# Stick-breaking heads: the keys' low parts queued behind a softplus' low part, and one multiplication moved to the end of a head's output

## The chip, the cores and the metric

The kernel runs on one core of a Trainium2 chip. The metric is the device time of one execution in microseconds (us). Every time below is from a run on the chip or from a hardware profile of one execution. The engines are named as in the profile: PE multiplies matrices (PEld is its weight load), DVE and ACT do elementwise work, POOL does elementwise work and masks, SP starts transfers.

## What is computed

The reference is one block of a hybrid encoder for 512 tokens and 16 learned meta tokens, 528 in all, of width 1024, in float32. A normalised input is projected once into all the parts; stick-breaking attention (8 heads of width 64) and gated linear attention (4 heads) run side by side, are merged by sigmoid gates, and a gated MLP follows. The change lies in the stick-breaking attention:

```python
z = jnp.einsum('bhqd,bhkd->bhqk', qi, k) * scale
u = jnp.where(strict, jax.nn.log_sigmoid(-z), 0.0)
tail = lax.cumsum(u, axis=3, reverse=True) - u
w = jnp.where(strict, jnp.exp(jax.nn.log_sigmoid(z) + tail), 0.0)
return jnp.einsum('bhqk,bhkd->bhqd', w, v)
```

So a head needs logits, a softplus of them, a running sum of that softplus over the keys, an exponential, and a product with the values.

## The kernel before

**Two-part numbers.** PE multiplies in a rounded format. To stay near float32, the kernel splits each operand into a high part (`h` at the end of the tile's name, a rounding copy) and a low part (`l`, the operand minus the high part), and adds up the products high by high, high by low and low by high. A high part in these heads is a CAST on DVE at L144, its low part a TENSOR_TENSOR at L145 (`split_v`). A product `z<-v0h,tri` is thus followed by its twin `z<-v0l,tri`.

**Stages.** The input is normalised; then come the four gated-linear heads, then the stick-breaking heads in four pairs (`for j in range(4)`), then the output projections and the MLP. For each pair the weights of three projections (`sk`, `sq`, `sv`: keys, queries and values, made by `sb_proj`, one pair ahead) and of four gate projections (`mg`, `go`, `mg`, `go`) arrive by transfer. ACT rounds each block of weights (L88, tile `wh_...`, 128x1024), and POOL makes its low part (L89, tile `wl_...`, 128x1024). The projections (`proj`, L113) are by far the most work on PE in this stage; the attention's own products lie between them.

**One pair.** `sb_parts` makes the operands of a pair's two heads: ACT rounds the keys and the scaled queries (`ks` L601, `qh` L603 and L605), DVE makes the low parts (`ks` L602, `ql` L604 and L606, 64x528, two of each a pair). `sb` then runs the keys in blocks of 128. First come the last 16 tokens and the first 16 for both heads together (tiles `zs`, `vs`, `ws`; `vs` is also the name of the split values), then block 3 for both heads (`z` of 288 columns), then for each head blocks 2, 1 and 0 (272, 400 and 512 columns). For a block PE makes the logits (`z`, L619), ACT takes three functions of them (`e`, L624 to L626), DVE makes the softplus (`v`, L628), POOL masks the diagonal (L632), DVE splits it (`v0h`, `v0l` for block 0), PE adds its running sum to `z` (L642) and sums it for the earlier blocks (`s`, L656), ACT takes the exponential (`w`, L646), POOL masks it, DVE multiplies in what the later blocks left over (L649) and splits the weights (`w0h`, `w0l`), and PE multiplies all weights with the values into the head's output `po` (L736 to L741). Before, that output begins with block 0, high and then low, and goes on with blocks 1, 2, 3 and the last tokens.

**What sets the order.** The program is written in the order of the text, and a list scheduler with a cost model of its own lays the instructions of all engines out in time; what it lays out is the order in which each engine then runs them, one after another. `tc.issue_after(x)` around an instruction tells it not to place that instruction ahead of x. On the chip each engine runs its list in order and waits by semaphores for operands and free buffers. So `sk`, `sq`, `sv` of the next pair and the operands of the next pair are laid out beside the second head of the pair before.

## Time and profile before

| | |
|---|---|
| median of 3 runs | 947.62 us (947.43 to 950.25) |
| the profiled execution's own time | 947.23 us |
| its span, first to last instruction | 945.5 us |
| PE busy | 920.3 us, 97% |
| DVE busy | 631.7 us, 67% |
| ACT busy | 492.3 us, 52% |
| POOL busy | 351.0 us, 37% |
| mean granted PE clock | 0.995 |

PE is busy nearly everywhere, so the time is PE's work and the moments at which PE stands still. A row of the profile's timeline has a start in us from the span's beginning, a duration in us, the engine, the line, the operation, `output<-inputs` by tile names, and shapes; `x2` says that a row stands for two instructions. A bracket at its end gives the idle time of the engine ahead of it and the instruction that ended that. The stick-breaking heads lie between about 250 and 474 us.

### The profile page before, as it was taken

How to read it: one execution, taken by the hardware profiler on the slowest of the kernel's cores; microseconds unless marked ns; L12 is line 12 of the kernel's file. 1: busy time of each engine (PE TensorE's matmuls, PEld its weight loads, DVE VectorE, ACT ScalarE, POOL GpSimd, SP SyncE). 2: the span in 40 equal slices, each digit the busy share in tenths (PEclk: the TensorE clock that was granted, in tenths of full speed). 3: DMA queues.
4: the chain of work that ended last, by engine and by line, in shares of the span. 5: the costliest groups of instructions: out<-in, count | busy, mean ns of one | idle time of the engine just before them, and what ended most of it. 6: DMA issues, size and time to landing. Idle time of an engine off the chain costs nothing.

```text
span 945.5 us, 17900 instructions
## 1 busy us (share of the span) xinstructions
PE 920.3 (97%) x7229; PEld 842.8 (89%) x7229; DVE 631.7 (67%) x1080; ACT 492.3 (52%) x934; POOL 351.0 (37%) x259
## 2 busy tenths in 40 slices
PE   7999999999999998999999998999999999999996
PEld 7999999999999997999998777999999999988785
DVE  6576858677558785887848438455544445488988
ACT  6674656556567674676663245533333333355654
POOL 5433232333355443554445331544444444101100
PEclk9999999999999999999999999999999999999998
DMA  7122222212223212221214642333333333274923
GB/s 221 46 69 68 69 68 68 68 47 72 64 73 85 62 52 68 67 82 54 73 53 122 232 141 96 101 101 90 89 90 98 102 90 90 90 267 154 266 81 123
DMA packets 129876, 93.39 MB, mean 99 GB/s; under 512 B 4080, under 2 KB 114930, under 8 KB 129794
## 3 DMA queue, kind: packets, MB, share of 16 engines
q1 hardware_dynamic: 126178, 82.55, 29.4%
q10 hardware_dynamic: 2112, 6.82, 2.0%
q0 software_dynamic: 1504, 2.88, 1.8%
q8 instruction: 57, 0.93, 0.4%
q14 instruction: 25, 0.20, 0.1%
HBM read 88.05 MB, written 4.19 MB: 98 GB/s over the span
## 4 chain that ended last, share of the span: by engine, by line
PE 86%; DVE 7%; issue 2%; ACT 2%; POOL 1%; DMA 0%; DVEq 0%; POOLq 0%; ACTq 0%
PE pt_up L113 13%; PE ga L915 12%; PE pt_gv L113 5%; PE pt_gr L113 5%; PE pt_mg L113 4%; PE pt_ms L113 4%; PE pt_go L113 4%; PE dA L1087 3%; PE dD L1087 3%; PE pt_gk L113 3%; PE wob L930 3%; PE pt_so L113 2%; PE pt_gq L113 2%; PE dB L1087 2%; PE wo L951 2%
## 5 line engine op out<-in xcount | busy, mean ns | idle before, releaser
L89 POOL TENSOR_TENSOR wl_ga<-raw_ga,wh_ga 128x1024 fp32r<-128x1024 f32 x22 | 55.3, 2518 | 74.3 <-ACT wh_ga L88 57.1
L89 POOL TENSOR_TENSOR wl_up<-raw_up,wh_up 128x1024 fp32r<-128x1024 f32 x22 | 52.9, 2407 | 79.4 <-ACT wh_up L88 79.4
L113 PE MATMUL pt_up<-h2h,wh_up 128*128 128x256 f32 (+1 forms) x352 | 73.1, 283 | 1.3 <-ACT h2h L140 1.3
L113 PE MATMUL pt_up<-h2l,wh_up 128*128 128x256 f32 (+1 forms) x352 | 73.3, 283 | 0.0
L113 PE MATMUL pt_up<-h2h,wl_up 128*128 128x256 f32 (+1 forms) x352 | 73.2, 282 | 0.0
L915 PE MATMUL ga<-h2h,wh_ga 128*128 128x512 f32 (+1 forms) x192 | 72.0, 376 | 0.7 <-ACT h2h L140 0.7
L915 PE MATMUL ga<-h2l,wh_ga 128*128 128x512 f32 (+1 forms) x192 | 72.1, 376 | 0.0
L915 PE MATMUL ga<-h2h,wl_ga 128*128 128x512 f32 (+1 forms) x192 | 72.1, 376 | 0.0
L88 ACT CAST wh_up<-raw_up 128x1024 fp32r<-128x1024 f32 x22 | 23.1, 1049 | 78.8 <-PE pt_up L113 75.0
L113 PEld LDWEIGHTS pt_up<-h2h,wh_up 128*128 128x128 f32 x352 | 56.8, 189 | 3.3 <-ACT h2h L140 1.6
L113 PEld LDWEIGHTS pt_up<-h2l,wh_up 128*128 128x128 f32 x352 | 55.5, 189 | 0.0
L113 PEld LDWEIGHTS pt_up<-h2h,wl_up 128*128 128x128 f32 x352 | 55.4, 189 | 0.0
L915 PEld LDWEIGHTS ga<-h2h,wl_ga 128*128 128x128 f32 x192 | 36.2, 188 | 7.0
L915 PEld LDWEIGHTS ga<-h2h,wh_ga 128*128 128x128 f32 x192 | 36.1, 188 | 7.0 <-ACT h2h L140 0.9
L915 PEld LDWEIGHTS ga<-h2l,wh_ga 128*128 128x128 f32 x192 | 36.1, 188 | 6.2
L1018 DVE SCALAR_TENSOR_TENSOR cy<-pt_up,cw,cy 128x511 f32<-128x511 f32 (+1 forms) x22 | 16.4, 745 | 36.5 <-ACT cy L1015 36.5
L88 ACT CAST wh_ga<-raw_ga 128x1024 fp32r<-128x1024 f32 x22 | 23.1, 1048 | 26.4 <-PE ga L915 25.2
L1018 DVE SCALAR_TENSOR_TENSOR yp<-pt_up,cw,yp 128x511 f32<-128x511 f32 (+1 forms) x22 | 16.4, 746 | 29.6 <-ACT yp L1015 29.6
L140 ACT CAST sh_p<-As 128x512 fp32r<-128x512 f32 (+1 forms) x30 | 17.4, 584 | 29.4 <-PE dB L1087 12.6
L89 POOL TENSOR_TENSOR wl_gr<-raw_gr,wh_gr 128x1024 fp32r<-128x1024 f32 x8 | 19.1, 2386 | 36.1 <-ACT wh_gr L88 27.2
L1115 POOL DMA_DIRECT2D tv<-in_w_ffn_down_dram x6 | 7.1, 1177 | 68.0 <-DVE wl_p L141 68.0
L113 PE MATMUL pt_gr<-hnh,wh_gr 128*128 128x258 f32 (+1 forms) x128 | 28.2, 294 | 0.0
(558 smaller groups left out, 3170.1 us busy)
## 6 DMA issues: line engine op xcount, KB each, us to landing
raw_up<-in_w_ffn_up_dram SPq DMA_DIRECT2D x22, 512.0 KB, 3.9
raw_ga<-in_w_ffn_gate_dram SPq DMA_DIRECT2D x22, 512.0 KB, 3.8
raw_t<-in_w_ffn_down_dram SPq DMA_DIRECT2D x10, 512.0 KB, 7.4
raw_gv<-in_w_in_dram SPq DMA_DIRECT2D x8, 512.0 KB, 3.9
raw_gr<-in_w_in_dram SPq DMA_DIRECT2D x8, 512.0 KB, 3.8
raw_mg<-in_w_in_dram SPq DMA_DIRECT2D x8, 512.0 KB, 3.8
raw_go<-in_w_gla_out_dram SPq DMA_DIRECT2D x8, 512.0 KB, 4.3
raw_ms<-in_w_in_dram SPq DMA_DIRECT2D x8, 512.0 KB, 4.0
```

What stands on the lines that cost most here:

```text
L88: act.copy(hi_out, raw)
L89: lo_eng.tensor_tensor(out=lo_out, in0=raw, in1=f32(hi_out), op=ALU.subtract)
L113: last_pr[0] = pe.matmul(dst, a[:, k, :], b[:, k, lo:hi], start=n == 0, stop=n == len(steps) - 1)
L140: act.copy(hi, src)
L915: last_mm[0] = pe.matmul(pt[:, lo:hi], a[:, k, :], b[:, k, lo:hi], start=lo == 0 and k == 0 and q == 0, stop=k == KT - 1 and q == 2, skip_ ...
L930: last_mm[0] = pe.matmul(pt, a, b, start=q == 0, stop=q == len(ops) - 1)
L951: last_mm[0] = pe.matmul(pos[i // 2][:, (i % 2) * 512 : (i % 2) * 512 + 512], m[k][:, t], w, start=k == 0 and q == 0, stop=k == 7 and q == 2)
L1018: dve.scalar_tensor_tensor(out=y[:, d:], in0=pt[:, : SEQ - d], scalar=c, in1=y[:, d:], op0=ALU.mult, op1=ALU.add)
L1087: mm[i] = pe.matmul(dsts[i], a, b, start=first and k == 0 and j == 0, stop=last and k == NP - 1 and j == 2, skip_group_check=True)
L1115: return lambda n, q, nk: pool.dma_start(out=t[:, q : q + nk, :], in_=block(s, c, q, nk), accum_op=ALU.add)
```

## The change

Two things are changed in the order of the work; no computation is added or taken out.

First, `parts` keeps the low part that it made last, and `sb` leaves behind the low part of the softplus of block 0 of its second head (`v0l`). When `sb_parts` makes the operands of the next pair, the two low parts of the keys (L602, now L606) may not be placed ahead of that `v0l`. For the first pair there is no such instruction, and nothing holds.

Second, in a head's output the second product, that with the low weights of block 0 (`w0l`), is moved to the end: `w0h`, blocks 1, 2 and 3, the last tokens, `w0l`.

```diff
@@ split_v
         dve.tensor_copy(hi, src)
-        dve.tensor_tensor(out=lo, in0=src, in1=f32(hi), op=ALU.subtract)
+        return dve.tensor_tensor(out=lo, in0=src, in1=f32(hi), op=ALU.subtract)
@@ sb_parts
                 act.copy(ks[o, hd, :], k[o])
-                dve.tensor_tensor(out=ks[n, hd, :], in0=k[o], in1=f32(ks[o, hd, :]), op=ALU.subtract)
+
+                with tc.issue_after(last_v[0].ins) if last_v[0] else ExitStack():
+                    dve.tensor_tensor(out=ks[n, hd, :], in0=k[o], in1=f32(ks[o, hd, :]), op=ALU.subtract)
@@ parts
-            split_v(hi[:rows, :n], lo[:rows, :n], src)
+            last_v[0] = split_v(hi[:rows, :n], lo[:rows, :n], src)
@@ sb
                     vp = parts(vi[:, :n], f"v{i}", nm, P, n, [P, n])
+                    low = last_v[0]
...
-                first = True
-                for i, t, wt in reversed(wts):
-                    for b in wt:
-                        pe.matmul(po[:, t - NM :], vs[:, i, hd, :], b, start=first, stop=False, skip_group_check=True)
-                        first = False
-                for b in w3:
-                    pe.matmul(po[:, 384 - NM :], vs[:, 3, hd, :], b[:, 144 * hd : 144 * hd + 144], start=False, stop=False, skip_group_check=True)
-                for b in ws:
-                    pe.matmul(po[:, 512 - NM :], vs[:16, 4, hd, :], b[:16, 32 * hd + 16 : 32 * hd + 32], start=False, stop=True, skip_group_check=True)
+                ops = [(t - NM, vs[:, i, hd, :], b) for i, t, wt in reversed(wts) for b in wt]
+                ops += [(384 - NM, vs[:, 3, hd, :], b[:, 144 * hd : 144 * hd + 144]) for b in w3]
+                ops += [(512 - NM, vs[:16, 4, hd, :], b[:16, 32 * hd + 16 : 32 * hd + 32]) for b in ws]
+                ops.append(ops.pop(1))
+                for q, (c, a, b) in enumerate(ops):
+                    pe.matmul(po[:, c:], a, b, start=q == 0, stop=q == len(ops) - 1, skip_group_check=True)
                 add_halves(hd, po, NM, 512)
             split_v(sbh[:, j, :], sbl[:, j, :], o32)
+            last_v[0] = low
```

No instruction is added or taken out on any engine. Since the scheduler lays everything out anew, the order moves on PE, DVE, ACT and POOL from the first pair's first output to the end of the stage; SP's order stays. Three places matter below. In the names `_1_` stands for the pair's second head.

The first is DVE at the end of the second pair, where the operands of the third pair (`ql`, `ks`) are made beside the second head's blocks 1 and 0. Before:

```order
L144 CAST v1h_1_4534<-v_1_4531 128x400
L707 TENSOR_TENSOR o_1_4318<-po_0_4480,lo_0_16_4491 64x512
L606 CAST ql_5003<-ql_5003 64x528 x2
L145 TENSOR_TENSOR v1l_1_4535<-v_1_4531,v1h_1_4534 128x400
L749 TENSOR_TENSOR tg<-pt_go_4951,lseg_4938 128x514
L602 TENSOR_TENSOR ks_5001<-raw_k_4594,ks_5001 64x528 x2
L628 SCALAR_TENSOR_TENSOR v_1_4561<-z_1_4554,e_1_4557 128x512
L649 TENSOR_TENSOR w_1_4540<-w_1_4540,E_1_4521 128x272
L144 CAST v0h_1_4564<-v_1_4561 128x512
L144 CAST w1h_1_4544<-w_1_4540 128x400
L145 TENSOR_TENSOR v0l_1_4565<-v_1_4561,v0h_1_4564 128x512
L145 TENSOR_TENSOR w1l_1_4545<-w_1_4540,w1h_1_4544 128x400
```

And now:

```order
L753 TENSOR_TENSOR tg<-pt_go_4951,lseg_4938 128x514
L610 CAST ql_5003<-ql_5003 64x528
L632 SCALAR_TENSOR_TENSOR v_1_4561<-z_1_4554,e_1_4557 128x512
L653 TENSOR_TENSOR w_1_4540<-w_1_4540,E_1_4521 128x272
L144 CAST w1h_1_4544<-w_1_4540 128x400
L144 CAST v0h_1_4564<-v_1_4561 128x512
L145 TENSOR_TENSOR w1l_1_4545<-w_1_4540,w1h_1_4544 128x400
L145 TENSOR_TENSOR v0l_1_4565<-v_1_4561,v0h_1_4564 128x512
L606 TENSOR_TENSOR ks_5001<-raw_k_4594,ks_5001 64x528 x2
```

The two `ks` went from ahead of the softplus `v` of block 0 to behind its low part `v0l`, and `w1h` and `w1l` came ahead of `v0l`. On ACT, at the same place, the rounding `wh_sq` (L88) went from ahead of the second function (L625) of that block's logits to behind it.

On PE, where that `v0h` and `v0l` are multiplied, the order before was this (`zs` are the third pair's first logits, which need `ks`; `pt_sq` is the query projection):

```order
L619 MATMUL zs_5029<-ql_5003,ks_5001 16x16
L113 MATMUL pt_sq_5368<-hnl,wh_sq_5364 128x272
L642 MATMUL z_1_4554<-v0h_1_4564,tri 128x512
L113 MATMUL pt_sq_5368<-hnl,wh_sq_5364 128x256
L113 MATMUL pt_sq_5368<-hnh,wl_sq_5365 128x272
L113 MATMUL pt_sq_5368<-hnh,wl_sq_5365 128x256
L113 MATMUL pt_sq_5368<-hnh,wh_sq_5364 128x272
L113 MATMUL pt_sq_5368<-hnh,wh_sq_5364 128x256
L113 MATMUL pt_sq_5368<-hnl,wh_sq_5364 128x272
L113 MATMUL pt_sq_5368<-hnl,wh_sq_5364 128x256
L642 MATMUL z_1_4554<-v0l_1_4565,tri 128x512
```

And now:

```order
L646 MATMUL z_1_4554<-v0h_1_4564,tri 128x512
L113 MATMUL pt_sq_5368<-hnh,wh_sq_5364 128x272
L113 MATMUL pt_sq_5368<-hnh,wh_sq_5364 128x256
L113 MATMUL pt_sq_5368<-hnl,wh_sq_5364 128x272
L113 MATMUL pt_sq_5368<-hnl,wh_sq_5364 128x256
L113 MATMUL pt_sq_5368<-hnh,wl_sq_5365 128x272
L113 MATMUL pt_sq_5368<-hnh,wl_sq_5365 128x256
L113 MATMUL pt_sq_5368<-hnh,wh_sq_5364 128x272
L113 MATMUL pt_sq_5368<-hnh,wh_sq_5364 128x256
L113 MATMUL pt_sq_5368<-hnl,wh_sq_5364 128x272
L646 MATMUL z_1_4554<-v0l_1_4565,tri 128x512
```

Ahead of `z<-v0h`, where the eight `zs` and one `pt_sq` stood since row 2476 of PE's list, there are now sixteen `pt_sq`; between the two `z` there are nine instead of seven; and the eight `zs` come four products behind `z<-v0l`.

The second place is DVE at the end of the third pair, where the fourth pair begins (`vs`, `ws` are its first softplus and weights). Before:

```order
L649 TENSOR_TENSOR w_1_5280<-w_1_5280,E_1_5261 128x400
L144 CAST wshs_5764<-ws_5761 16x64
L144 CAST w0h_1_5284<-w_1_5280 128x512
L145 TENSOR_TENSOR wsls_5765<-ws_5761,wshs_5764 16x64
L145 TENSOR_TENSOR w0l_1_5285<-w_1_5280,w0h_1_5284 128x512
L749 TENSOR_TENSOR tg<-pt_go_6082,lseg_6069 128x514
```

And now:

```order
L144 CAST v0h_1_5274<-v_1_5271 128x512
L145 TENSOR_TENSOR w1l_1_5255<-w_1_5250,w1h_1_5254 128x400
L145 TENSOR_TENSOR v0l_1_5275<-v_1_5271,v0h_1_5274 128x512
L606 TENSOR_TENSOR ks_5711<-raw_k_5304,ks_5711 64x528 x2
L157 TENSOR_SCALAR tg<-pt_mg_6020 128x514
L161 TENSOR_TENSOR lseg_6069<-tg,lseg_6069 128x514
L653 TENSOR_TENSOR w_1_5280<-w_1_5280,E_1_5261 128x400
L144 CAST w0h_1_5284<-w_1_5280 128x512
L145 TENSOR_TENSOR w0l_1_5285<-w_1_5280,w0h_1_5284 128x512
L632 SCALAR_TENSOR_TENSOR vs_5752<-zs_5739,es_5748 16x64
L753 TENSOR_TENSOR tg<-pt_go_6082,lseg_6069 128x514
L144 CAST vsh_5755<-vs_5752 16x64
```

`ks` moved behind `v0l` here too, and `w1l` ahead of it; the split of `ws` is no longer between `w0h` and `w0l`; the softplus `vs` and its split, which stood ahead of this stretch, now follow `w0l`. On PE the fourth pair's `zs` moved 58 rows later.

The third place is PE at the last output, that of the fourth pair's second head. Before, six products of the gate projection `pt_ms` lie between `w0h` and `w0l`, the last two of them shown:

```order
L113 MATMUL pt_ms_6519<-hnh,wh_ms_6515 128x258
L113 MATMUL pt_ms_6519<-hnh,wh_ms_6515 128x256
L736 MATMUL po_1_5998<-w0l_1_5995,vs_5726 128x512
L736 MATMUL po_1_5998<-w1h_1_5964,vs_5726 128x400
L736 MATMUL po_1_5998<-w1l_1_5965,vs_5726 128x400
L736 MATMUL po_1_5998<-w2h_1_5934,vs_5726 128x272
```

And now:

```order
L744 MATMUL po_1_5998<-w0h_1_5994,vs_5726 128x512
L744 MATMUL po_1_5998<-w1h_1_5964,vs_5726 128x400
L744 MATMUL po_1_5998<-w1l_1_5965,vs_5726 128x400
L744 MATMUL po_1_5998<-w2h_1_5934,vs_5726 128x272
L744 MATMUL po_1_5998<-w2l_1_5935,vs_5726 128x272
L744 MATMUL po_1_5998<-w3h_5795,vs_5726 128x144
L744 MATMUL po_1_5998<-w3l_5796,vs_5726 128x144
L744 MATMUL po_1_5998<-wshs_5764,vs_5726 128x16
L744 MATMUL po_1_5998<-wsls_5765,vs_5726 128x16
L744 MATMUL po_1_5998<-w0l_1_5995,vs_5726 128x512
```

The output's ten products now stand together, six rows later than before with `w0h` and eight rows later with `w0l`.

## The prediction

> **What bounds the kernel now.** I read the page's first lines, then the windows of the stick-breaking stage, then PE's waits in it, and last the timelines of the places where PE waits.

> ```profile
> span 945.5 us, 17900 instructions
> PE 920.3 (97%) x7229; PEld 842.8 (89%) x7229; DVE 631.7 (67%) x1080; ACT 492.3 (52%) x934; POOL 351.0 (37%) x259
> ...
> 250.00:474.00 224.00, 217.80 (x1683) 209.89 (x1682) 169.45 (x274) 145.59 (x285) 107.16 (x113) 0.99 0.25 68
> 360.00:362.00 2.00, 2.00 (x9) 1.91 (x10) 0.98 (x4) 0.60 (x1) 0.53 (x2) 0.50 0.77 212
> 362.00:363.00 1.00, 1.00 (x6) 1.00 (x6) 1.00 (x5) 0.00 (x0) 0.00 (x0) 0.50 0.34 100
> 363.00:364.00 1.00, 1.00 (x9) 1.00 (x8) 0.30 (x1) 0.00 (x0) 0.00 (x0) 0.86 0.00 0
> ...
> PE z L642 <- DVE v0l L145: 2.3, 1, 2.3
> PE po L736 <- DVE w0l L145: 1.4, 2, 0.9
> PE z L642 <- DVE v0h L144: 1.0, 1, 1.0
> PE zs L619 <- ACT qh L605: 0.9, 1, 0.9
> PE po L736 <- DVE w0h L144: 0.4, 1, 0.4
> ```

> The stage that the change lays out anew, 250 to 474 us, is PE's: busy 217.80 of 224.00 us, so it stands still for 6.2 us, and the five waits (total, times, longest) name 6.0 of them. The number behind POOL's in a window is the granted clock: for some 3.3 us behind 360 it was half, then 0.86 of full. PE is busy in those windows and yet loses 2 x 0.50 + 0.50 + 0.14 = 1.64 us. So all that can be won here is 6.2 + 1.64 = 7.8 us, 0.8% of the time; the 0.9 at `qh` lies ahead of the change. Everything else in the stage is work of PE, which the change does not touch.

> **The third pair's place.** These are PE, DVE, POOL and ACT around the longest wait:

> ```profile
> 354.13 0.41 PE L113 MATMUL pt_sq<-hnh,wl_sq 128*128 128x272 f32 x2
> 354.38 0.41 PE L113 MATMUL pt_sq<-hnh,wh_sq 128*128 128x272 f32 x2
> 354.62 0.17 PE L619 MATMUL zs<-qh,ks 128*16 128x16 f32 x1
> ...
> 356.20 0.50 PE L642 MATMUL z<-v0h,tri 128*128 128x512 f32 x1 [1.00 <-DVE v0h L144]
> ...
> 359.80 0.78 PE L642 MATMUL z<-v0l,tri 128*128 128x512 f32 x1 [2.27 <-DVE v0l L145]
> ```

> ```profile
> 350.87 3.53 DVE L602 TENSOR_TENSOR ks<-raw_k,ks 64x528 fp32r<-64x528 f32 x2
> 354.43 0.69 DVE L628 SCALAR_TENSOR_TENSOR v<-z,e 128x512 f32<-128x512 f32 x1
> ...
> 355.64 0.51 DVE L144 CAST v0h<-v 128x512 fp32r<-128x512 f32 x1 [0.17 <-POOL v L632]
> ...
> 356.91 2.84 DVE L145 TENSOR_TENSOR v0l<-v,v0h 128x512 fp32r<-128x512 f32 x1
> 359.67 0.56 DVE L145 TENSOR_TENSOR w1l<-w,w1h 128x400 fp32r<-128x400 f32 x1
> ```

> ```profile
> 351.39 2.43 POOL L89 TENSOR_TENSOR wl_sq<-raw_sq,wh_sq 128x1024 fp32r<-128x1024 f32 x1 [4.97 <-ACT wh_sq L88]
> 355.25 0.35 POOL L632 TENSOR_SCALAR_AFFINE_SELECT v<-v 128x112 f32<-128x112 f32 x1 [1.43 <-DVE v L628]
> ...
> 355.84 0.93 POOL L730 TENSOR_TENSOR E<-E,E 128x272 f32<-128x272 f32 x1
> 356.73 2.47 POOL L89 TENSOR_TENSOR wl_sv<-raw_sv,wh_sv 128x1024 fp32r<-128x1024 f32 x1
> ```

> ```profile
> 350.25 1.05 ACT L88 CAST wh_sq<-raw_sq 128x1024 fp32r<-128x1024 f32 x1
> 351.21 0.62 ACT L625 ACTIVATE e<-e 128x512 f32<-128x512 f32 x1
> 351.87 0.63 ACT L626 ACTIVATE e<-e 128x512 f32<-128x512 f32 x1
> ```

> The two `ks` took 3.53 us, since one of them lay across POOL's `wl_sq`; `v`, whose operand ACT had ready at 352.50, came at 354.43. Then `v0l` lay across `wl_sv` and took 2.84 us. A DVE row of this kind that begins during a POOL `wl` ends about 0.55 us behind it (`v0l` at 359.75, `wl_sv` at 359.20); I call that held. PE waits 1.00 + 2.27 us, and then the half clock costs 1.64: 4.9 us in all.

> What becomes of it: PE reaches `z<-v0h` sixteen products later than the old `zs`, at 354.62 + 16 x 0.12 = 356.5 (354.13 to 354.62 hold four). But four things run against that. (1) ACT now takes L625 (0.66 from start to start) ahead of `wh_sq`, so `wl_sq` runs from about 352.05 to 354.5, and PE asks for it at 354.13: a new wait of 0.35. (2) POOL masks `v` only behind `wl_sq`, with one more mask of 0.29 ahead, so at 355.15 instead of 355.60; DVE's gain of 2 us on `v` shrinks to 0.45 there, and `v0h` is done at about 355.9, a microsecond ahead of PE (356.9). No wait. (3) `w1l` now stands ahead of `v0l`. `wl_sv` begins behind that mask and `E`, at about 355.95, just ahead of `w1l`, which is held to about 358.9; `v0l` (0.6) follows to 359.5. PE asks for it at 356.9 + 0.24 + 9 x 0.12 = 358.2: 1.3 us. (4) The two `ks` (0.70 each when not held: 3.53 less a held 2.83) end at 360.2 and 360.9, and PE asks for the second at about 360.5: 0.4. Together 2.0 us, in three pieces over 6.8 us, where today 3.27 fall into 4.6 us. I take it that the clock stays: 4.9 - 2.0 = **2.9 us won**. The ends: 4.9 if nothing waits, and nothing if the half clock stays and `v0l` comes no earlier.

> **The second and the fourth pair.**

> ```profile
> 307.14 2.39 POOL L89 TENSOR_TENSOR wl_mg<-raw_mg,wh_mg 128x1024 fp32r<-128x1024 f32 x1 [0.51 <-ACT wh_mg L88]
> ...
> 307.15 2.66 DVE L144 CAST w0h<-w 128x512 fp32r<-128x512 f32 x1
> ...
> 413.61 0.69 DVE L145 TENSOR_TENSOR v0l<-v,v0h 128x512 fp32r<-128x512 f32 x1
> ...
> 420.62 2.40 DVE L145 TENSOR_TENSOR wsls<-ws,wshs 16x64 fp32r<-16x64 f32 x1
> 422.95 0.67 DVE L145 TENSOR_TENSOR w0l<-w,w0h 128x512 fp32r<-128x512 f32 x1
> ```

> ```profile
> 413.67 2.88 POOL L89 TENSOR_TENSOR wl_mg<-raw_mg,wh_mg 128x1024 fp32r<-128x1024 f32 x1 [0.38 <-ACT wh_mg L88]
> ...
> 416.56 0.39 PE L642 MATMUL z<-v0l,tri 128*128 128x512 f32 x1
> ...
> 423.68 0.50 PE L736 MATMUL po<-w0l,vs 128*128 128x512 f32 x1 [0.86 <-DVE w0l L145]
> ```

> At the second pair `ks` moves 1.4 us of work behind `v0l`, ahead of `w0h`; but `w0h` is held to the end of `wl_mg` anyway and would be up to 0.9 us later at its start. **Zero**; the wait of 0.4 stays.

> At the fourth pair the wait of 0.86 goes, because `wsls`, held for 2.40, no longer stands ahead of `w0l`. But today `v0l` begins 0.06 us ahead of `wl_mg`. With `w1l` (0.56) ahead of it, it begins inside and is held to 416.55 + 0.55 = 417.1; PE asks at about 416.55: 0.55 lost. The `ks` follow to 418.5, and the second half of `zs` is asked for at about 418.1: 0.4. Then `vsh` stands behind `w0l` and `tg`, while the next `wl_go` may begin as soon as `vs` is masked: held, it is 0.7 to 1 us late for PE. Against 0.86 today these 1.65 to 2 make **a loss of about 0.8 us**, with ends of 0.86 won and 2.5 lost (one more hold).

> **The last output, and the rest.**

> ```profile
> 468.83 2.77 DVE L145 TENSOR_TENSOR w0l<-w,w0h 128x512 fp32r<-128x512 f32 x1
> ...
> 470.02 0.39 PE L736 MATMUL po<-w0h,vs 128*128 128x512 f32 x1
> ...
> 471.65 0.50 PE L736 MATMUL po<-w0l,vs 128*128 128x512 f32 x1 [0.53 <-DVE w0l L145]
> ...
> 473.18 0.50 PE L113 MATMUL pt_ms<-hnl,wh_ms 128*128 128x258 f32 x2
> ```

> The output begins six products later (470.7), and `w0l` is asked for behind `w0h` (0.3) and the eight smaller ones (473.18 - 471.65 less 0.3, 1.2 us): about 472.2, behind its end at 471.60. **0.5 won**, with 0 as the other end. In the other outputs of the stage nothing but these waits for `w0l` and the one for `w0h` is listed, and the number of products is the same, so moving `w0l` there is worth nothing. The fourth pair's own blocks are laid out anew over some 40 us in which PE waits for nothing today. I charge 0.4 us for them, between zero and one held DVE row that PE then lacks (2.77 - 0.67 = 2.1).

> The sum: 2.9 - 0.8 + 0 + 0.5 - 0.4 = 2.2 us won. The profiled execution took 947.23 us (span 945.5 and 1.7 around it), which makes 945.0; the median of the runs is 0.4 above it: **about 945.3 us**.

> **The rivals.** (A) *All waits go.* If `v0l` gets through ahead of `wl_sv`, nothing is held in the third pair, and the clock stays: 4.9 + 0.86 + 0.5 = 6.3 won, 941.3 us. For it: PE asks so much later. Against it: POOL's list puts the mask of `v` behind `wl_sq` and `wl_sv` right behind.

> (B) *The hold is handed on, and little changes.* `ks` was late because of `wl_sq`, not for its own 1.4 us; take it out of the way, and the next DVE row with two operands meets the next `wl`. If `v0l` then ends where it does today plus a late `wl_sq`, PE waits 0.35 + 2.3 + 0.4 and the clock falls again (1.64): 4.7 of 4.9, and with the other terms 0.5 lost, about 948. The rows at 350.87, 356.91 and 420.62 speak for it. [...]

> (C) *Slower: `ks` itself is held, with `zs` right behind.* `zs` now stands four to five products, 0.5 to 0.6 us, behind `z<-v0l` in the third and fourth pairs, so a hold of 2.1 us on a `ks` goes to PE nearly whole. In both, that is 4.2 on top of what I counted (less the 0.8 for `ks` there), and one fall of the clock, 1.64: 5.0 lost against 2.2 won, 950.4 us. It decides from two holds on; one hold alone leaves no change. For it: 3.53 for `ks` today. Against it: a hold of `w1l` or `v0l` by the same `wl` lets `ks` go free behind it.

> **How the numbers follow.** The forecast has 0.50, A 0.17, B 0.18, C 0.15. What a measurement here can tell from no change is about 0.3%, 2.8 us. Faster by more than that: A, and the forecast's upper part (its own range is 943 to 947.3; beyond 2.8 won lie some 0.46 of it): 0.17 + 0.23 = 0.40. Slower: the worse half of C, 0.08, and 0.05 for stalls of the new order that no case names, 0.13. Same: 0.47. The range for 8 in 10 reaches nearly to A and past B: 941.8 to 948.9.

> **What would show it.** Right: no half clock near 360; the wait at `z<-v0l` in the third pair down to 1 to 1.5 us; small new waits of `pt_sq` for `wl_sq` and of `zs` for `ks` (L606); a wait for `vsl` or `vsh` at the fourth pair's start; none for `w0l`. The mechanism is wrong if `v0l` takes 0.69 us there and nothing waits (A), if the clock is at 0.50 again (B), or if `ks` has rows near 2.8 us with PE waiting for them (C). A loss in the fourth pair's own blocks over 2 us would make the charge of 0.4 wrong.

## The result, and the profile after

The changed kernel takes 954.25 us (median of 5 runs, 952.59 to 955.50), the kernel before beside it 948.64: a ratio of 1.0061, with a 95% interval of 1.0043 to 1.0079. It is 5.6 us slower; forecast were 945.3 us and a range that ended at 948.9. One more execution of the changed kernel, when it was run again, took 2276 us at full clock and is left out of its figures. These are the first lines of the page of the changed kernel:

```profile
span 953.8 us, 17903 instructions
PE 927.7 (97%) x7229; PEld 849.1 (89%) x7229; DVE 626.7 (66%) x1080; ACT 490.8 (51%) x934; POOL 350.4 (37%) x259
```

The span grew by 8.3 us, from 945.5 to 953.8, and PE's busy time by 7.4, although PE runs the same 7229 products (the three more instructions are semaphore instructions of DVE and ACT). The growth is larger than the 5.6 us between the medians because the profile caught the longest of the five executions here, 955.5 us, and a short one before. Products that take longer point to the clock. In the windows of the changed kernel (the number behind POOL's is the granted clock) there are now three stretches below full speed while PE works, where before had one; behind PE's last product both kernels have one more, which holds up no product:

```profile
256.00:258.00 2.00, 2.00 (x12) 2.00 (x12) 0.00 (x0) 0.99 (x2) 1.43 (x1) 0.57 0.00 0
258.00:260.00 2.00, 2.00 (x14) 1.93 (x13) 0.00 (x0) 1.08 (x5) 0.94 (x1) 0.58 0.00 0
314.00:324.00 10.00, 10.00 (x41) 9.00 (x42) 4.92 (x13) 1.79 (x4) 1.30 (x4) 0.52 0.19 53
324.00:326.00 2.00, 2.00 (x14) 1.75 (x14) 0.28 (x1) 1.65 (x4) 0.52 (x1) 0.86 0.00 0
597.00:598.00 1.00, 0.99 (x7) 0.99 (x8) 0.77 (x2) 0.07 (x1) 0.00 (x0) 0.81 0.00 0
598.00:600.00 2.00, 2.00 (x11) 2.00 (x11) 0.69 (x1) 0.59 (x1) 0.00 (x0) 0.50 0.00 0
600.00:601.00 1.00, 1.00 (x7) 1.00 (x7) 0.00 (x0) 0.00 (x0) 0.00 (x0) 0.50 0.00 0
```

Each row loses its length times what its clock lacks to 1.00: 1.7 us behind 256, 5.1 behind 314, 1.7 behind 597, 8.5 in all against 1.6 before. By this count that is 6.8 of the 8.3 us; the second profile, below, shows that the count is about 0.9 too high. The stretch at 360 us, which the change was forecast to remove, is gone; the one at 314 is new, and it is the longest. The waits of PE in the stick-breaking stage (total, times, longest):

```profile
PE z L646 <- DVE v0l L145: 2.2, 2, 1.1
PE po L744 <- DVE w0h L144: 2.0, 1, 2.0
PE zs L623 <- ACT qh L609: 0.9, 1, 0.9
PE pt_go L113 <- POOL wl_go L89: 0.3, 1, 0.3
PE pt_sq L113 <- POOL wl_sq L89: 0.3, 1, 0.3
PE zs L646 <- DVE vsh L144: 0.3, 1, 0.3
PE pt_sv L113 <- ACT raw_k L331: 0.3, 1, 0.3
PE zs L623 <- DVE ks L606: 0.2, 1, 0.2
```

Their sum is 6.5 us, little more than before (6.0). The old waits for `v0h` and `w0l` went, and a wait of 2.0 us for `w0h` came. It is at the second pair. These are rows of the timeline there:

```profile
305.87 1.44 DVE L606 TENSOR_TENSOR ks<-raw_k,ks 64x528 fp32r<-64x528 f32 x2
...
307.40 0.60 ACT L331 COPY raw_k<-pt_sk 128x528 f32<-128x528 f32 x1 [5.49 <-DVE ks L606]
...
309.15 1.07 ACT L88 CAST wh_mg<-raw_mg 128x1024 fp32r<-128x1024 f32 x1
...
310.30 2.54 POOL L89 TENSOR_TENSOR wl_mg<-raw_mg,wh_mg 128x1024 fp32r<-128x1024 f32 x1 [0.17 <-ACT wh_mg L88]
...
310.53 2.75 DVE L653 TENSOR_TENSOR w<-w,E 128x400 f32<-128x400 f32 x1
...
313.38 0.43 DVE L144 CAST w0h<-w 128x512 fp32r<-128x512 f32 x1
...
313.86 0.51 PE L744 MATMUL po<-w0h,vs 128*128 128x512 f32 x1 [2.01 <-DVE w0h L144]
```

Two things happen. The low parts `ks` (L606), now behind `v0l`, still read `raw_k`; ACT's copy of the next keys into the same buffer stands still for 5.49 us until they are done, and the exponentials and `wh_mg` queue behind it. And DVE reaches its last row ahead of `w0h` (L653) 0.23 us after POOL began `wl_mg`: that row is held to 313.28 where it takes 0.57 to 0.65 us when free. PE, out of other work, waits 2.01 us.

The waits elsewhere, PE's rows in the third and fourth pair and behind the stage:

```profile
362.80 0.51 PE L113 MATMUL pt_sq<-hnh,wl_sq 128*128 128x272 f32 x2 [0.33 <-POOL wl_sq L89]
...
367.90 0.50 PE L646 MATMUL z<-v0l,tri 128*128 128x512 f32 x1 [1.06 <-DVE v0l L145]
...
369.37 0.18 PE L623 MATMUL zs<-qh,ks 128*16 128x16 f32 x1 [0.18 <-DVE ks L606]
...
418.13 0.51 PE L113 MATMUL pt_go<-oh,wl_go 128*128 128x258 f32 x2 [0.33 <-POOL wl_go L89]
...
423.25 0.50 PE L646 MATMUL z<-v0l,tri 128*128 128x512 f32 x1 [1.13 <-DVE v0l L145]
...
430.90 0.20 PE L646 MATMUL zs<-vsh,tri 16*16 16x64 f32 x1 [0.31 <-DVE vsh L144]
...
502.07 0.50 PE L113 MATMUL pt_so<-sbh,wh_so 128*128 128x258 f32 x2 [0.54 <-DVE min L157]
```

Pair by pair they come to this. Second pair: 1.6 more for `w0h`, 0.3 for the copy. Third: 1.57 for 3.27, 1.7 less. Fourth: 1.77 for 0.86, 0.9 more. Last output: 0.5 less. Behind the stage: 0.54 and another 0.2 (for `m`), 0.8 more. Together 1.4 more.

### The profile page after: what moved, and what is told of

It is laid out like the page before. It is cut to its first block, busy times and chain, and to the rows that moved or that the text cites. A ratio compares the mean times of both kernels' runs of the same rounds, so it can differ in the third digit from the quotient of the medians.

```text
span 953.8 us, 17903 instructions
## 1 busy us (share of the span) xinstructions
PE 927.7 (97%) x7229; PEld 849.1 (89%) x7229; DVE 626.7 (66%) x1080; ACT 490.8 (51%) x934; POOL 350.4 (37%) x259
## 3 DMA queue, kind: packets, MB, share of 16 engines
q0 software_dynamic: 1504, 2.88, 1.8%
## 4 chain that ended last, share of the span: by engine, by line
PE 87%; DVE 6%; ACT 3%; issue 2%; DMA 1%; POOL 0%; DVEq 0%; ACTq 0%; POOLq 0%
PE pt_up L113 13%; PE ga L919 12%; PE pt_gv L113 5%; PE pt_mg L113 5%; PE pt_gr L113 5%; PE pt_go L113 4%; PE pt_ms L113 4%; PE dA L1091 3%; PE dD L1091 3%; PE pt_sv L113 3%; PE pt_gk L113 3%; PE pt_sk L113 2%; PE pt_gq L113 2%; PE dB L1091 2%; PE wo L955 2%; PE wob L934 2%
## 5 line engine op out<-in xcount | busy, mean ns | idle before, releaser
L89 POOL TENSOR_TENSOR wl_up<-raw_up,wh_up 128x1024 fp32r<-128x1024 f32 x22 | 52.9, 2406 | 80.9 <-ACT wh_up L88 80.9
L89 POOL TENSOR_TENSOR wl_ga<-raw_ga,wh_ga 128x1024 fp32r<-128x1024 f32 x22 | 55.1, 2510 | 74.5 <-ACT wh_ga L88 57.4
L113 PE MATMUL pt_up<-h2h,wh_up 128*128 128x256 f32 (+1 forms) x352 | 73.4, 284 | 1.3 <-ACT h2h L140 1.3
L113 PE MATMUL pt_up<-h2h,wl_up 128*128 128x256 f32 (+1 forms) x352 | 73.3, 282 | 0.0
L113 PE MATMUL pt_up<-h2l,wh_up 128*128 128x256 f32 (+1 forms) x352 | 73.3, 283 | 0.0
L88 ACT CAST wh_up<-raw_up 128x1024 fp32r<-128x1024 f32 x22 | 23.1, 1049 | 79.4 <-PE pt_up L113 76.3
L113 PEld LDWEIGHTS pt_up<-h2h,wh_up 128*128 128x128 f32 x352 | 57.0, 190 | 3.3 <-ACT h2h L140 1.6
L113 PEld LDWEIGHTS pt_up<-h2l,wh_up 128*128 128x128 f32 x352 | 55.5, 189 | 0.0
L113 PEld LDWEIGHTS pt_up<-h2h,wl_up 128*128 128x128 f32 x352 | 55.4, 189 | 0.0
L88 ACT CAST wh_ga<-raw_ga 128x1024 fp32r<-128x1024 f32 x22 | 23.1, 1048 | 26.8 <-PE ga L919 25.5
L89 POOL TENSOR_TENSOR wl_gr<-raw_gr,wh_gr 128x1024 fp32r<-128x1024 f32 x8 | 19.1, 2386 | 36.0 <-ACT wh_gr L88 27.1
L113 PE MATMUL pt_gr<-hnh,wh_gr 128*128 128x258 f32 (+1 forms) x128 | 28.2, 294 | 0.0
```

Of the source, the lines that this page charges most:

```text
L88: act.copy(hi_out, raw)
L89: lo_eng.tensor_tensor(out=lo_out, in0=raw, in1=f32(hi_out), op=ALU.subtract)
L113: last_pr[0] = pe.matmul(dst, a[:, k, :], b[:, k, lo:hi], start=n == 0, stop=n == len(steps) - 1)
```

## The experiments

Fourteen kernels, each with the runs of the kernel before on the same chip beside it. "Low parts free" means that the `ks` rows may be placed anywhere, as before. Nothing is left out of the computation in any of them. The kernel before had medians of 947.50 to 948.49 us on the four chips used, so rows are compared by their ratios where their chips differ.

| kernel | median, us | ratio to before | 95% interval |
|---|---|---|---|
| the change, again | 952.60 | 1.0038 | 1.0024 to 1.0052 |
| only the low parts queued | 949.11 | 1.0006 | 0.9995 to 1.0017 |
| only `w0l` last | 942.69 | 0.9942 | 0.9928 to 0.9957 |
| `w0l` last, low parts queued for pair 2 only | 948.30 | 0.9992 | 0.9978 to 1.0006 |
| the same, pair 3 only | 944.90 | 0.9963 | 0.9949 to 0.9977 |
| the same, pair 4 only | 944.47 | 0.9960 | 0.9946 to 0.9974 |
| change, two buffers for `raw_k` | 946.65 | 0.9985 | 0.9977 to 0.9994 |
| change, that `wl_mg` on DVE | 947.70 | 0.9998 | 0.9987 to 1.0009 |
| change, both cures | 945.92 | 0.9974 | 0.9964 to 0.9984 |
| before, two buffers for `raw_k` | 946.44 | 0.9982 | 0.9974 to 0.9991 |
| `w0l` last in the last output only | 948.15 | 0.9998 | 0.9988 to 1.0008 |
| `w0l` last in one output of pair 2 only | 944.98 | 0.9962 | 0.9948 to 0.9976 |
| `w0l` last, last `wl_sv` on DVE | 941.19 | 0.9928 | 0.9915 to 0.9941 |
| the same, two buffers for `raw_k` | 938.94 | 0.9909 | 0.9894 to 0.9924 |

### The change once more

No edit.

> The changed kernel, nothing altered. Theory T (the ACT copy of the next keys, L331, waits 5.5 us for the delayed low part of the keys, so that w0h comes 2 us late at the second pair; this wait, and where it lies against windows of 3.41 us in which the clock is set, costs 1.6 us of waiting and 5.1 us of half clock): median within 2 us of 954.3; the copy waits 5 to 6 us again and PE about 2 us for w0h; half clock again behind it, unless a window boundary cuts the wait in two. The stretches of half clock at 256 and 597 us, behind waits that the kernel before has too, may be gone or others may be there: they follow the position of the windows, which I take to be another one in each execution. Rival D (the clock follows the order of the program alone): the same three stretches at the same places.

Measured: 952.60 us, over 11 runs 947.74 to 954.66, and the time goes with the mean granted clock: 947.74 at 0.999, 949.65 and 949.70 at 0.996, 952 to 955 at 0.994 to 0.990. The profile caught one of the short executions, a span of 947.9 us. Its windows at the second pair, and PE's wait there:

```profile
310.00:312.00 2.00, 0.48 (x4) 0.27 (x3) 1.90 (x1) 0.92 (x3) 1.47 (x1) 1.00 0.00 0
312.00:314.00 2.00, 1.51 (x9) 1.38 (x9) 1.87 (x6) 0.00 (x0) 0.47 (x2) 1.00 0.66 189
314.00:316.00 2.00, 2.00 (x15) 1.73 (x15) 1.77 (x5) 1.17 (x2) 0.18 (x1) 1.00 0.24 73
316.00:324.00 8.00, 8.00 (x60) 7.43 (x59) 5.01 (x10) 5.34 (x13) 3.34 (x4) 1.00 0.07 17
```

```profile
312.49 0.51 PE L744 MATMUL po<-w0h,vs 128*128 128x512 f32 x1 [2.01 <-DVE w0h L144]
```

The wait is the same to a hundredth, 2.01 us, and the clock stays at 1.00. The stretch at 256 is gone too; one lies at 592 to 595 us. So rival D falls: the same instructions with the same waits run 5.9 us apart in span, and the difference is the clock. What the order alone costs can now be read: 947.9 less one stretch of 1.7 is 946.2, before 945.5 less its one is 943.8. So 2.4 of the 8.3 us are the order's, and the half clock made the other 5.9, in some executions more than in others. The waits listed above name 1.4 of the 2.4; where PE loses the other 1.0 was not found. And the count of 6.8 for the half clock was too high: `po<-w0h` starts at 313.86 in the first profile and at 312.49 here, 1.37 us apart, where the stretch ahead of it counts 1.7; the one counted 5.1 cost the other 4.5 of the 5.9.

### One half of the change at a time

Only the low parts:

```diff
-                ops.append(ops.pop(1))
```

> Only the keys' low parts are queued behind v0l; w0l stays second in an output. Theory T: the copy of the keys waits 5 to 6 us at the second pair as in the whole change, PE 1.5 to 2.5 us for w0h and up to 0.7 more for w0l; 953 to 956 us. Rival W (w0l as the last product, or what it does to the order of later stages, makes the kernel slower): no slower than 949.5.

Only `w0l` last:

```diff
-                with tc.issue_after(last_v[0].ins) if last_v[0] else ExitStack():
+                with ExitStack():
```

> Only w0l is moved to the end of an output; the keys' low parts are free as before. Theory T: the copy of the keys waits for nothing, no half clock at the second pair, the wait for v0l in the third pair (2.3 us) and its half clock as before; 947.5 to 949.5 us. Rival W: 952 or more.

Measured: 949.11 and 942.69 us. Both miss what theory T expected. Rival W's time for the first came, but `w0l` last alone is 5.8 us *faster*, where the prediction gave it 0.5, at the last output; so W falls with the second. Its profile lists 2.3 us of PE's waits in place of 6.0 and no half clock at 360 (two `pt_sq` products in 0.25 us at 361.00 to 362.97, where the kernel before took 0.44), 5.3 us together; its mean clock over 250 to 474 us is 0.99 all the same. The queued low parts alone make no difference that can be measured, although their profile has ACT's wait of 5.6 us, a wait of 1.9 for `w0h` and a mean clock of 0.98 over 250 to 474 us, by which some 4.5 us are lost. The two edits do not add up: with the low parts free, `w0l` last gains 5.8 us; with them queued, it costs 3.5 (952.60 against 949.11). Of these, 0.8 are the waits behind the stage, which the profile with queued low parts alone does not have; the rest was not taken apart. Beside the better kernel the queued low parts cost 9.9 us.

### The low parts queued for one pair

`w0l` last, and in place of `if last_v[0]`:

```diff
-                with tc.issue_after(last_v[0].ins) if last_v[0] else ExitStack():
+                with tc.issue_after(last_v[0].ins) if j in (1,) else ExitStack():
```

and in the same way `(2,)` and `(3,)`.

> w0l last as in the change, and the keys' low parts queued behind v0l for the second pair alone. Against the kernel with w0l last alone (942.7 us) this moves seven rows of DVE and four of ACT, all at the second pair. Theory T2 (the second pair is the expensive place: the two low parts, 1.4 us, push DVE's rows into POOL's wl_mg and hold ACT at raw_k for 5 to 6 us, PE then waits about 2 us for w0h, and in most executions half clock of up to three windows follows, 5.1 us): 946 to 949.5 us, with a wait of 1.5 to 2.5 us for w0h and one to three windows of half clock behind it. Rival P34 (the loss comes from the third and fourth pair or from the order of later stages): 944 or less.

> w0l last, and the keys' low parts queued behind v0l for the third pair alone, the place for which the prediction forecast the gain. Theory T2: ACT waits 6 us at raw_k there too, but PE comes later; the wait for v0l stays at 1 to 1.4 us since w1l or v0l is held by wl_sv either way: 942 to 945 us, no gain over w0l last alone (942.7). If the prediction's own reading holds (the low parts stand in the way of v0l): 941 or less. Rival P34: 946 or more.

> w0l last, and the keys' low parts queued behind v0l for the fourth pair alone. No further keys are projected behind it, so ACT waits for nothing at raw_k. Theory T2: new waits of 0.3 to 1 us (vsh, v0l or ks): 942.5 to 945 us. Rival P34: 946 or more.

Measured: 948.30, 944.90 and 944.47 us. Beside `w0l` last alone (0.9942) the ratios say 0.0050 more for the second pair, 0.0021 for the third, 0.0018 for the fourth: 4.7, 2.0 and 1.7 us. Added to 0.9942 they make 1.0031; the whole change, run beside it, made 1.0038. So, with `w0l` last, the pairs' parts add up within their intervals; each of the two smaller ones is hardly beyond its own. T2's times hold, and its main point: the second pair is the dear place, with a wait of 2.00 us for `w0h` in its profile and half clock behind it (312 to 314 us at 0.85, 314 to 322 at 0.50, 322 to 324 at 0.59: some 10.2 us at half). At the third pair, for which the change was made, queueing the low parts gains nothing over `w0l` last: it makes 2.4 us of waits for `v0l` at two places where that kernel has 1.4 at one. At the fourth, the waits that T2 expected for `vsh`, `v0l` or `ks` did not come; the profile has two others behind the stage, 0.5 and 0.2.

### Which of two delays makes `w0h` late

ACT's copy, freed by a second buffer:

```diff
-            t = pst_.tile([P, T], F32, tag=nm, name=f"raw_{nm}{j}")
+            t = pst_.tile([P, T], F32, tag=nm, name=f"raw_{nm}{j}", bufs=2 if nm == "k" else 1)
```

> The whole change, and two buffers in place of one for the copy of the keys (raw_k), so that ACT has not to wait for the low parts of the last keys. Theory T: no wait of ACT at raw_k; the exponentials of blocks 1 and 0 come 3 to 5 us earlier, wh_mg too, and PE waits 0 to 0.6 us for w0h at the second pair, with no three windows of half clock: 6 to 7 us less than the changed kernel, 947 to 949 us. Rival H (the row of DVE held by POOL's wl_mg is the cause, whatever ACT does): the hold falls on w0h or the row ahead of it all the same, PE waits 1.5 us or more, and the time stays at 952 or above.

The hold, taken away by giving that one low part to DVE:

```diff
-            pt = proj(load_w(cols(w_in, C_MGLA + j * P), KT, f"mg{j}"), hnh, hnl, LATE, f"mg{j}")
+            pt = proj(load_w(cols(w_in, C_MGLA + j * P), KT, f"mg{j}", lo_eng=dve if j == 2 else pool), hnh, hnl, LATE, f"mg{j}")
```

> The whole change, and DVE instead of POOL makes the low part of the one weight tile (wl_mg) that held DVE's row at the second pair; it then stands behind w0h on DVE. Theory H (the hold is what makes w0h late): the row of L653 takes 0.6 to 0.7 us in place of 2.75, PE waits at most 0.5 us for w0h and there is no half clock behind it, although ACT still waits 5 to 6 us at raw_k; w0l comes 1.1 us later, which its last place covers in part: 946 to 949 us. Theory T (ACT's wait at raw_k alone makes it late): PE still waits 1.5 us or more, 951 or above.

Measured: 946.65 and 947.70 us. Beside the change run again the ratios say 0.0053 and 0.0040 less, 5.0 and 3.8 us. By the time alone either could be the cause. The timelines tell them apart. With two buffers ACT waits no more, and the hold has only gone to another row, `w1l`:

```profile
305.35 2.39 POOL L89 TENSOR_TENSOR wl_mg<-raw_mg,wh_mg 128x1024 fp32r<-128x1024 f32 x1 [0.72 <-ACT wh_mg L88]
305.47 2.70 DVE L145 TENSOR_TENSOR w1l<-w,w1h 128x400 fp32r<-128x400 f32 x1
308.09 0.56 DVE L653 TENSOR_TENSOR w<-w,E 128x400 f32<-128x400 f32 x1
308.76 0.43 DVE L144 CAST w0h<-w 128x512 fp32r<-128x512 f32 x1
...
309.24 0.50 PE L744 MATMUL po<-w0h,vs 128*128 128x512 f32 x1 [1.71 <-DVE w0h L144]
```

With `wl_mg` on DVE, ACT still waits 5.49 us, and PE does not wait for `w0h` at all:

```profile
305.72 0.60 ACT L331 COPY raw_k<-pt_sk 128x528 f32<-128x528 f32 x1 [5.49 <-DVE ks L606]
...
308.85 0.57 DVE L653 TENSOR_TENSOR w<-w,E 128x400 f32<-128x400 f32 x1
309.52 0.43 DVE L144 CAST w0h<-w 128x512 fp32r<-128x512 f32 x1
...
310.03 0.47 PE L744 MATMUL po<-w0h,vs 128*128 128x512 f32 x1
```

Theory T, that ACT's wait makes `w0h` late, falls; the hold makes it late (H). Of H's forecasts for two buffers the wait came, but not the time of 952 or above; the next section asks why. The same row takes 0.57 us instead of 2.75 once `wl_mg` is off POOL.

### Why two buffers help all the same

Both edits together, and the two buffers in the kernel before, where no low part is delayed:

> The whole change with both cures of the second pair: two buffers for raw_k, and DVE in place of POOL for that wl_mg. If the hold is all of the loss there and ACT's wait costs nothing by itself: the time of the kernel with the one cure (947.7), within 1 us. If ACT's wait of 5.5 us costs something of its own: 944 to 946.5.

> The kernel before with two buffers for the keys' copy and nothing else; DVE and POOL keep their order. If that cure only removes the old wait at 254 us: PE's wait of 0.9 us for qh goes, with the half clock that follows it in some executions, and the time is 1.3 to 2.5 us under the kernel before. If the cure works at the second pair, on what the change does there: no difference over 0.5 us here.

Measured: 945.92 and 946.44 us. By the ratios that is 2.3 us under the one cure (0.0024) and 1.7 under the kernel before (0.0018). In both profiles PE's wait of 0.9 us for `qh` at 254 us is gone, which has nothing to do with the change; in the changed kernel's first profile a stretch of half clock follows that wait, 1.7 us, and in its second, as in the kernel before's, none. So the gain is, by the author's estimate, mostly that wait and, where it comes, its half clock. The 0.6 between the two gains, which is what is left for ACT's wait by itself, lies within their intervals; 0.3 us of PE is listed for the copy. What two buffers saved beyond the 1.7 in the changed kernel, some 3 to 4 us, was not measured apart. The wait for `w0h` is 0.3 us shorter with them, and the 11 runs have mean clocks of 0.994 to 0.999, those of the change 0.990 to 0.999: fewer stretches of half clock. That the shorter wait is the reason is argued, not shown.

### Where `w0l` last gains

In the last output only, and in the output of the second pair's first head only:

```diff
-                ops.append(ops.pop(1))
+                if (j, hd) == (3, 1):
+                    ops.append(ops.pop(1))
```

and the same with `(1, 0)`; low parts free in both.

> The keys' low parts are free, and w0l is the last product in the very last output only (fourth pair, second head). DVE, ACT and POOL keep the order of the kernel before; only rows of PE move. The prediction's step (0.5 won there, since the wait of 0.53 for that w0l goes) expects 947.0 to 948.0 with before at 947.5 to 948.5. If w0l's own place is what gained 5.8 in the kernel with w0l last in all outputs: 945 or less.

> The keys' low parts are free, and w0l is the last product only in the output of the second pair's first head, which lies 10 us ahead of the long waits at the third pair. Theory L (the gain of w0l last is not in the product's own place but in the new layout behind it, in which the low parts of the keys and the softplus v end ahead of POOL's wl_sq): the waits of 1.0 and 2.3 us for v0h and v0l fall together to 1.5 or less, and the half clock behind them goes: 944 to 946 us. The prediction's step (moving w0l elsewhere is worth nothing): 947.5 to 949.

Measured: 948.15 and 944.98 us. At the last output the wait of 0.53 us goes, as predicted, and the time shows no difference. In the output of the second pair, where no product waited, the move is worth 3.5 us: theory L. Behind that output the scheduler laid DVE out anew, and the rows at the third pair now read:

```profile
351.18 0.70 DVE L606 TENSOR_TENSOR ks<-raw_k,ks 64x528 fp32r<-64x528 f32 x1
...
352.26 0.70 DVE L606 TENSOR_TENSOR ks<-raw_k,ks 64x528 fp32r<-64x528 f32 x1
...
353.37 2.41 POOL L89 TENSOR_TENSOR wl_sq<-raw_sq,wh_sq 128x1024 fp32r<-128x1024 f32 x1 [5.20 <-ACT wh_sq L88]
...
353.86 0.69 DVE L632 SCALAR_TENSOR_TENSOR v<-z,e 128x512 f32<-128x512 f32 x1 [0.90 <-ACT e L630]
```

The `ks` are done 0.4 us before `wl_sq` begins, free, 0.70 each; before, one lay across it. PE's waits there fall from 1.00 and 2.27 to one of 1.5, 1.8 us less. That the 1.6 us of half clock behind them are gone too, which would make up the gain, is the author's estimate; the clock there was not shown. What queueing the low parts was to bring, this order has without it.

### A version that beats both

`w0l` last, low parts free, and the one low part that still held a row (`w1l`, 2.76 us, ahead of `v0l`) given to DVE; then two buffers for `raw_k` as well:

```diff
-            act.copy(t, proj(load_w(cols(w_in, c0 + j * P), KT, f"s{nm}{j}"), hnh, hnl, ALL, f"s{nm}{j}"))
+            act.copy(t, proj(load_w(cols(w_in, c0 + j * P), KT, f"s{nm}{j}", lo_eng=dve if nm == "v" and j == 3 else pool), hnh, hnl, ALL, f"s{nm}{j}"))
```

> w0l last in all outputs, the keys' low parts free, and for the last pair's value weights DVE in place of POOL makes the low part (wl_sv, that held w1l for 2.76 us and so kept v0l). Theory H (the hold is the cause): w1l takes about 0.6 us, the wait of 1.45 us for v0l goes to 0.2 or less, DVE has 1.1 us more work behind v0l which PE does not wait for: 940.5 to 942 us, under both kernels. Otherwise (the 1.1 us on DVE makes a new wait): 942.5 to 944.

> w0l last in all outputs, the keys' low parts free, DVE in place of POOL for the last wl_sv, and two buffers for the keys' copy. If the cures add up: 941.2 less 1.3 to 2.5, 938.5 to 940 us, with no wait of PE over 0.3 us left between 245 and 480 us. If not: 941 to 942.

Measured: 941.19 and 938.94 us, 0.9928 and 0.9909 of the kernel before. Beside `w0l` last alone (0.9942) the first gain lies within the intervals, but its trace shows what H expected: `w1l` takes 0.56 us, and the wait for `v0l` is gone. In the stage of the second kernel PE is busy for 219.94 of 220 us, and no wait is listed in it:

```profile
250.00:470.00 220.00, 219.94 (x1726) 213.43 (x1726) 162.81 (x280) 147.86 (x289) 106.59 (x113) 1.00 0.25 70
```

## Why the prediction was wrong, step by step

**Third pair: right, in each of its parts.** Forecast were waits of 0.35 for `wl_sq`, none for `v0h`, 1.3 for `v0l`, 0.4 for `ks`, and full clock, with `w1l` held; measured 0.33, none, 1.06, 0.18, and 1.00, with `w1l` at 2.75. Instead of 2.9 us it won 3.3 (1.7 of waits and the 1.6 of half clock).

**Fourth pair: right in the sum, by luck.** Forecast was a loss of 0.8: 0.86 gone against 0.55 for `v0l`, 0.4 for `ks` and 0.7 to 1 for `vsh`. Measured were 1.13, 0 and 0.31, and 0.33 for `wl_go` that was not foreseen: 1.77 against 0.86, a loss of 0.9. The row that was held is not the one the prediction named: it let `w1l` pass and held `v0l`, but `w1l` took 2.77 us, and `v0l` came a row behind it, in 0.68.

**Last output: right in the trace** (0.53 gone), too small to see in the time. **The charge of 0.4 for the rest** was made for the fourth pair's own blocks, where no wait came; the 0.8 behind the stage was not foreseen.

**Second pair: the step that failed.** The prediction put it at zero, since "`w0h` is held to the end of `wl_mg` anyway and would be up to 0.9 us later at its start". That moves `w0h` alone. The rows ahead of it move with it, and the last of them stood close to `wl_mg`, which began at 307.14:

```profile
306.40 0.65 DVE L649 TENSOR_TENSOR w<-w,E 128x400 f32<-128x400 f32 x1
```

Of the prediction's own 0.9 us, 0.74 bring this row into `wl_mg`. In the changed kernel the hold fell on it (L653, 2.75 us), and `w0h`, which needs its result, came behind its end: a wait of 0.4 became one of 2.0. With two buffers, where ACT's copy stands still for nothing, the hold fell one row earlier, on `w1l`, and PE still waited 1.71. So the step that failed is which row is held.

The prediction also did not ask who else waits for `ks`: ACT's copy does, since it needs the buffer that `ks` reads (the copy ran at 300.30 us in the kernel before, and at 307.40 now). That makes `wh_mg` and `wl_mg` later, but the two waits, 2.01 and 1.71, put its share at 0.3 us; at the third pair the copy stands still for even longer, 6.5 us, and PE has no wait for it.

**The price of a wait.** The forecast let the clock stay, and its rivals B and C let it fall once, for 1.64 us. The new wait brought a stretch three times as long in the first profile (10.24 us against 3.41), none in the second. The range of 941.8 to 948.9 had no room for that. (The last addition of the forecast, 945.0 and 0.4, makes 945.4, not 945.3; nothing hangs on it.)

**"Moving `w0l` there is worth nothing": also wrong**, on the other side. The product's own place was priced, not the order that the scheduler makes behind it; alone, the move is worth 5.8 us. The two errors met in one kernel: some 5.8 won by one edit, some 10 lost when the other is added.

**The rivals.** B's mechanism (the hold is handed on to the next row) acted in all three pairs: at the third, for which it was written, at the forecast's price and without B's fall of the clock, at the second at a price that nobody named. C forecast slower, with `ks` held; slower came, but no row of `ks` was held in the changed kernel (0.70 for each). In these runs a new order of DVE alone mostly moved the hold, from `ks` and `v0l` to L653 or to `w1l`, and where the one POOL instruction beside it was taken away the row ran free (2.75 to 0.57, 2.76 to 0.56 us). Not every row beside a `wl` is held: in the kernel before, `v` (354.43, 0.69 us) ran while POOL did nothing; in the changed kernel the same row (360.83, 0.69 us) lies inside `wl_sq` (360.34 to 362.74) and is free. And a held row need not have two operands, as B has it: the CAST `v0h` of the changed kernel took 2.62 us at 302.50, beside `wl_sv` (302.08 to 304.82), where the CAST `w0h` of the same size takes 0.43. Why a row is held was not shown.

## What to carry to other kernels

When a row is moved later on its engine, every row behind it moves too: ask of each of them, and not only of the one another engine waits for, what it now meets. List also who waits for a buffer that the moved row reads, though here that wait, 5.5 us of ACT, cost PE little. The place that pays can lie in another pair than the place that was mended. Here a new order mostly handed the hold of a row on to the next one, and moving the one POOL instruction beside it to DVE took the hold away in both places where it was tried (2.75 to 0.57 us, 2.76 to 0.56). With a scheduler that lays everything out anew, price each edit by the whole new order, and run each alone: here one edit of two was worth 0.6% and the other hid it.

## What the runs showed of the hardware

```profile
256.20:256.40 0.20, 0.20 (x4) 0.20 (x3) 0.00 (x0) 0.20 (x1) 0.00 (x0) 0.71 0.00 0
...
314.20:314.40 0.20, 0.20 (x2) 0.20 (x1) 0.20 (x1) 0.00 (x0) 0.00 (x0) 0.77 0.76 120
...
597.60:597.80 0.20, 0.20 (x4) 0.20 (x3) 0.17 (x2) 0.00 (x0) 0.00 (x0) 0.54 0.00 0
```

A row at 0.71 was at half for 0.58 of its length, so the falls are at 256.28, 314.31 and 597.62 us. In the same way it rises at 259.70 (259.60 to 259.80 at 0.76), 324.55 (324.40 to 324.60 at 0.63) and 601.03 us (601.00 to 601.20 at 0.93). The falls lie 58.03 and 283.3 us apart, 17.0 and 83.0 times 3.413 us, and the stretches are 1, 3 and 1 times 3.413 us long. In the kernel before the clock falls at 359.86 and 940.12 us (359.80 to 360.00 at 0.65, 940.00 to 940.20 at 0.81), 170.0 times 3.413 us apart. Counted back from the first of these in 31 steps of 3.4133 us, an estimate, a boundary lies at 254.05 us, inside the wait for `qh` (0.89 us, to 254.29), and the clock there stayed at 1.00.

**What PE did ahead of a fall.** These are the windows of 3.41 us, counted from the falls, ahead of and in the half clock of that profile (PE's busy time and its products come first):

```profile
252.87:256.28 3.41, 2.27 (x19) 1.76 (x18) 2.90 (x6) 3.32 (x6) 0.00 (x0) 1.00 0.24 72
310.90:314.31 3.41, 1.40 (x10) 1.14 (x10) 3.27 (x3) 1.39 (x5) 1.94 (x1) 1.00 0.07 18
314.31:317.72 3.41, 3.41 (x15) 3.06 (x14) 2.02 (x8) 0.58 (x1) 0.65 (x2) 0.50 0.47 135
317.72:321.14 3.42, 3.42 (x15) 2.82 (x15) 1.66 (x3) 0.80 (x2) 0.08 (x1) 0.50 0.00 0
321.14:324.55 3.41, 3.41 (x17) 3.34 (x16) 0.93 (x3) 0.61 (x2) 0.57 (x2) 0.50 0.02 5
594.20:597.62 3.42, 1.39 (x11) 1.03 (x10) 3.38 (x11) 1.30 (x4) 0.00 (x0) 1.00 0.10 38
```

Summing the columns of the products that start in a window: 2,880, 2,496 and 1,408 in the three that a fall followed, with PE idle for 1.14, 2.01 and 2.03 us. In the kernel before, the window ahead of the fall at 359.86 has 2,352 columns and 2.27 us of idle time. At half clock, 2,544 and 3,040 were followed by half clock again, 4,000 by full, and so were 3,888 at 256.28, 3,972 at 597.62 and, in the kernel before, 3,696 at 359.86. Between 245 and 925 us of these two profiles the other windows at full clock have 3,584 columns or more, and no fall came behind them; one exception, with 1,552 columns and 1.56 us of idle time (kernel before, 571.48 to 574.89), had no fall behind it and is not explained. Four falls are too few to tell whether columns or idle time decide: 1.14 us of idle time were followed by one (252.87), 1.09 us were not (577.14, 3,584 columns). The products right behind the wait at 254 us had 16 or 144 columns. PE did not stand still in the windows at 314.31 and 317.72 (busy for 3.41 and 3.42 us, at 0.50), and half clock followed each.

**So a wait's price is partly chance.** In the two profiles of the changed kernel the falls lie at different places (256.28, 314.31 and 597.62 us in the first, 591.84 in the second). Counted back from the stretch that begins at 591.84 in 82 steps of 3.4133 us, an estimate, the second profile has a boundary at 311.95; it cuts the wait of 2.01 us (310.48 to 312.49) in two, and the clock stayed at 1.00. In the first the wait lay inside one window, 310.90 to 314.31, and 10.24 us of half clock followed. That the boundary made the difference is the author's estimate from these two profiles.
